# One encoder layer on one core: the second norm's sums one product later, two additions of a down visit on GpSimd, one scaling tied in VectorE's order

## The chip, the core and the metric

The kernel runs on one core of a Trainium2 chip. A core has TensorE (matmuls, results in the eight PSUM banks), VectorE (DVE in the profile), ScalarE (ACT), GpSimd (POOL) and SyncE (SP, which here only issues transfers); each works through its own queue in order, and they wait for one another by semaphores. The metric is the device time of one execution in microseconds (us); the time of a kernel is the median of its runs.

## The reference

One layer of an encoder on 1024 tokens of width 1024, in float32: a norm, a projection, a pooling mixer beside chunked attention, an output projection; then a norm, a gated MLP of width 2816, and a gated input embedding; a last norm. The part that the change touches is the MLP:

```python
hn = rmsnorm(h, norm_ffn_g[i])          # y * rsqrt(mean(y*y) + EPS) * g
up = hn @ w_up[i]                       # (1024, 1024) @ (1024, 2 * 2816)
gt, val = up[..., :D_FF], up[..., D_FF:]
gt = causal_dwconv(gt, conv_w[i], conv_b[i])
h = h + (jax.nn.gelu(gt, approximate=False) * val) @ w_down[i]
```

## The kernel before, in words

**Layout.** Features lie on the 128 partitions, tokens along the free axis. The residual is H[0] to H[7], eight tiles of 128 features by 1024 tokens; HS[0] and HS[1] are the two halves of 512 tokens. Every float32 operand of a matmul is kept as a high part (ScalarE writes it, L141, in a rounded format) and a low part (VectorE writes the rest, L142), and each product is three matmuls (mm3, L136 to L138): high by high, high by low, low by high. `split` is this pair of operations.

**Up projection.** Block fi (0 to 21) is 128 gate columns and 128 value columns of w_up. Its four sub-products (gate or value, first or second token half) over the two halves of the input features are computed with seven products in place of eight, numbered 1 to 7, from sums and differences of the weight halves (`summed`, L893) and of the activations (forms). `step(fi, n)` runs product n: twelve matmuls into one of the banks x, y, z, w, then what must be read from it. For blocks 0 and 1 the banks are firsts[0] = (0, 3, 5, 4) and firsts[1] = (2, 3, 1, 5). Product 1 leaves its result in bank x; `seed` (L984, ScalarE) copies it, negated, into bank y as the start of products 6 and 7, and product 2 then goes on accumulating in bank x. After product 3 the gate's convolution follows: L1005 and L1006 on VectorE, the taps of L1031 on ScalarE, L1034 and L1035 on VectorE, then GELU on ScalarE (L1036). After product 7 VectorE takes one half of the values from PSUM (L1013), after product 4 the other (L1016, the scaling: values times the norm's factor). `product` splits the weights of three products ahead, into a ring of three buffers, so the split for product i + 3 waits until product i has been run.

**The second norm.** Its factor for a token is a power of the mean square. `Norm.add` squares a tile on ScalarE and adds it up on VectorE (L815), `sums` adds over the partitions with four matmuls by a column of ones (L821; the profile lists eight records), followed by a small VectorE operation (L824) and a power on GpSimd (L825); `rows` turns the result into rows with four transposes on TensorE (L829). norm_a is that of the first token half, norm_b of the second. The last squares of norm_b are added up when the output projection ends, directly ahead of the first up products, which are written at L1057 to L1063: (0,1), (1,1), norm_b.sums(), (0,2), (0,5). norm_b.rows() is called after product (0,3).

**Down projection.** It is done in groups g of four blocks, also with seven products, numbered 1, 2, 5, 4, 6, 7, 3 in their order. Each is called a visit here: `down_next` runs 24 matmuls into banks 4 to 7, adds the four results to the residual (L1236), and has the next visit's operands split (`split_next`; where the sign is negative by `split_last`, L1187 on ScalarE and L1188 on VectorE). Visits are hooked between the products of `up`. Their operands are sums and differences of gated tiles, which SyncE loads into buffers "one" and "grow" from memory (L1165) and GpSimd's transfers accumulate onto (L1163). Visit (4,5) falls into block 20, after product 3. Before its matmuls two additions (L1227, one for each of its j) add the "grow" tiles, of which (4,5) has already split its parts, onto the "one" tiles, the raw operands of the next visit, (4,4). The accumulating transfers into "grow" for visit (4,6) come after these reads. (4,4) is run in block 21, after product 1; between (4,5) and it lie the products (20,4) and (21,1).

**What sets the order.** TensorE's order is that of the program (`manual_schedule`). In this part of the kernel the other engines' orders are made when the kernel is built, by a planner that gives each engine the first ready instruction in the order of writing, by its own estimate of times; `high_priority(AHEAD)` moves an instruction 60 places forward in that order. `keep_in_program_order(i)` ties instruction i behind the last instruction written for its engine before it. The additions L1227 are tied this way, and so are the splits of (4,4), except for the high parts L1187.

Of the kernel before, what the change touches and what calls it, by code (L numbers as in the profile page):

```python
# [9 lines left out]
ALU = mybir.AluOpType  # L10
# [91 lines left out]
def trunk(tc, x0, xT, xn, pT, vecs, w_qk0, w_in, w_v, bias, counts, pool_w, w_out, w_up, w_down,  # L102
          w_gate, w_ple, out):
    nc = tc.nc
    act, dve, pe, pool, sp = nc.scalar, nc.vector, nc.tensor, nc.gpsimd, nc.sync

    with tc.tile_pool(name="sb", bufs=1) as sb, \
# [8 lines left out]
        PS = pp.tile([P, 8, 512], F32, name="PS")  # L116
# [6 lines left out]
        def r(kb, n):  # L123
            if kb >= 128:
                return B[:, int((kb - 128) * KW):int((kb - 128) * KW) + n]
            return R[:, int(kb * KW):int(kb * KW) + n]

        def f(kb, n):
            return F[:, int(kb * KW):int(kb * KW) + n]
# [4 lines left out]
        def mm3(ps, ahi, alo, bhi, blo, first, last, more=False):  # L134

            pe.matmul(ps, ahi, bhi, start=first, stop=False, skip_group_check=more)  # L136
            pe.matmul(ps, ahi, blo, start=False, stop=False, skip_group_check=more)  # L137
            pe.matmul(ps, alo, bhi, start=False, stop=last, skip_group_check=more)  # L138
# [22 lines left out]
        V = r(64, 8192).rearrange("p (k h c) -> p k h c", k=NTOK, h=N_HEADS)  # L161
# [623 lines left out]
        HS = [slice(0, 512), slice(512, 1024)]  # L785
# [59 lines left out]
        V = v_pool.__enter__().tile([P, SEQ], F32, name="V")  # L845
# [16 lines left out]
        rst = f(44, SEQ)  # L862
# [63 lines left out]
        def product(bank, first):  # L926

            i = done[0]
            prepare(i + 1)
            form = forms[order[i][1]]  # L930
            w_ = wu[i % 3]
            for k in range(4):
                mm3(PS[:, bank], w_[:, 0, k], w_[:, 1, k], *form[k], first and k == 0, k == 3, not first)
            done[0] += 1
            prepare(i + 4)
# [42 lines left out]
        def keep(dst, bank, scale=1.0):  # L978
            with tc.high_priority(AHEAD):
                act.activation(dst, PS[:, bank], AF.Copy, scale=scale)  # L980

        def seed(to, bank, scale=1.0):
            with tc.high_priority(AHEAD):
                act.activation(PS[:, to], PS[:, bank], AF.Copy, scale=scale)  # L984

        def step(fi, n):

            x, y, z, w = firsts.get(fi, (0, 1, 2, 3))
            product({1: x, 2: x, 5: z, 3: z, 6: y, 7: y, 4: w}[n], n in (1, 5) or n == 4 and fi < 2)
            if n == 1 and fi != 1:  # L990
                seed(y, x, -1.0)
            elif n == 2 and fi:
                gate0(x)
                if fi in halved[1:]:
                    gate(fi, HS[0])
            elif n == 5:
                keep(p5, z)
            elif n == 6:
                keep(u2, y)
                if fi == 1:  # L1000
                    gate(fi, HS[0], True)
            elif n == 3:
                if fi == 0:
                    norm_b.rows(rst[:, HS[1]])
                dve.tensor_tensor(G2, PS[:, z], u2, ALU.subtract)  # L1005
                dve.tensor_tensor(G2, G2, rst[:, HS[1]], ALU.mult)  # L1006
                gate(fi, HS[1] if fi in halved else slice(0, SEQ))
            elif n == 7:
                if fi > 1:
                    seed(w, y)  # L1010
                else:
                    keep(V[:, HS[0]], y)
                dve.tensor_tensor(V[:, HS[1]], PS[:, y], p5, ALU.subtract)  # L1013
            elif n == 4:
                if fi > 1:
                    dve.tensor_tensor(V[:, HS[0]], PS[:, w], rst[:, HS[0]], ALU.mult)  # L1016
                else:
                    dve.tensor_tensor(V[:, HS[0]], PS[:, w], V[:, HS[0]], ALU.add)
                    dve.tensor_tensor(V[:, HS[0]], V[:, HS[0]], rst[:, HS[0]], ALU.mult)

        def gate0(bank):
            dve.tensor_tensor(Gb[:, 2:2 + 512], PS[:, bank], rst[:, HS[0]], ALU.mult)

        def gate(fi, ts, pinned=False):

            a, b = ts.start, ts.stop
            y = Yb[:, ts]

            def cw(j):
                return vec[:, C_CW + j * NF + fi:C_CW + j * NF + fi + 1]  # L1030
            taps = act.activation(y, Gb[:, 2 + a:2 + b], AF.Identity, bias=vec[:, C_CB + fi:C_CB + fi + 1], scale=cw(2))  # L1031
            if pinned:
                tc.keep_in_program_order(taps)
            dve.scalar_tensor_tensor(y, Gb[:, 1 + a:1 + b], cw(1), y, ALU.mult, ALU.add)  # L1034
            dve.scalar_tensor_tensor(y, Gb[:, a:b], cw(0), y, ALU.mult, ALU.add)  # L1035
            act.activation(y, y, AF.Gelu)  # L1036
# [17 lines left out]
        def store(dst, ts=slice(0, SEQ)):  # L1054
            split(Yb[:, ts], dst[:, ts], dst[:, 1024 + ts.start:1024 + ts.stop])

        step(0, 1)  # L1057
        step(1, 1)
        norm_b.sums()
        step(0, 2)  # L1060
        for k in range(4):
            put(3, k, b22[k])
        step(0, 5)  # L1063
# [53 lines left out]
        raws, pairs = {}, {}  # L1117
# [77 lines left out]
        def split_next(pinned=False, held_back=False):  # L1195
            if nsplit[0] == len(sequence) or nsplit[0] > ndown[0]:
                return
            g, n = sequence[nsplit[0]]
            if not all((side, g, n) in asked for side in "wa"):
                return  # L1200
            nsplit[0] += 1
            pinned = pinned or (g, n) == (4, 4)
            for side in "wa":
                sign = -1.0 if side == "a" and n in NEGATIVE else 1.0
                for j in range(2):
                    t = raws[side, buffer(side, n), j]
                    hi, lo = pairs[side, j]
                    if sign > 0:
                        split(t, hi, lo, pinned)
                    else:  # L1210
                        last_piece.append((side, g, n, j, pinned))
                        if not (held_back and j):
                            split_last()
                if not last_piece:
                    split_done.add((side, g, n))
            ask()

        def down_next():

            g, n = sequence[ndown[0]]  # L1220
            ndown[0] += 1
            assert nsplit[0] == ndown[0]
            if (g, n) == (4, 5):
                assert ("a", 4, 4) in asked
                for j in range(2):
                    t = raws["a", "one", j]
                    tc.keep_in_program_order(dve.tensor_tensor(t, t, raws["a", "grow", j], ALU.add))  # L1227
            fresh = n in (1, 5, 6, 7)
            for d in range(4):
                for j in range(2):  # L1230
                    (whi, wlo), (ahi, alo) = pairs["w", j], pairs["a", j]
                    ds_ = slice(d * P, (d + 1) * P)
                    mm3(PS[:, 4 + d], whi[:, ds_], wlo[:, ds_], ahi, alo, fresh and j == 0, j == 1, not fresh)
                to, h = {1: (4, 1), 5: (4, 1), 6: (4, 1), 7: (4, 1), 2: (0, 0), 4: (4, 0), 3: (0, 1)}[n]
                t = H[to + d][:, HS[h]]
                dve.tensor_tensor(t, t, PS[:, 4 + d], ALU.subtract if n in (1, 5) else ALU.add)  # L1236
            if n == 1 and g < 4:
                put_off[0] = 3
            else:
                split_next()  # L1240
# [306 lines left out]
```

## Time and profile before

| what | value |
|---|---|
| median of 3 runs | 1113.71 us (1113.18 to 1114.12) |
| the profiled execution | 1113.26 us |
| its span, first to last instruction | 1111.5 us |
| TensorE clock granted | 0.998 |
| TensorE busy | 1103.6 us, 99% |
| VectorE busy | 846.9 us, 76% |
| ScalarE busy | 579.4 us, 52% |
| GpSimd busy | 166.3 us, 15% |

The profile is of one execution. All times of the views are microseconds from the first instruction. A row of a timeline has the start, the duration, the engine, the line of the kernel, the operation with its result and inputs (R, BQ and TB hold operands in SBUF, F and RW float32 tiles in SBUF, PS is PSUM, Yd the gated tiles in memory), the shape, and in brackets how long the engine stood idle before it and who ended that. Matmuls overlap: one is shown as 0.39 us long, but they start about 0.23 us apart, so time on TensorE is read from start to start. The spans of GpSimd are rough.

### The profile page before, as it was taken

The numbers are of one execution on the slowest core, as the hardware profiler recorded it, in microseconds if no ns is written. First come the engines' busy times: TensorE is split into PE (matmuls) and PEld (weight loads), VectorE is DVE, ScalarE is ACT, GpSimd is POOL, SyncE is SP. The second block draws the span as 40 slices with busy tenths as digits, with TensorE's granted clock in tenths as the row PEclk, the third lists the DMA queues.
The fourth block names the chain that finished last, engine by engine and source line by source line (L and its number), as shares of the span: only waits on it lengthen the run. The fifth ranks groups of instructions, "written<-read, shape, count | busy, mean of one in ns | idle before, by whom it ended". The sixth has DMA issues, their size and how long they took to land.

```text
span 1111.5 us, 15629 instructions
## 1 busy us (share of the span) xinstructions
PE 1103.6 (99%) x5651; PEld 918.5 (83%) x5651; DVE 846.9 (76%) x1435; ACT 579.4 (52%) x1022; POOL 166.3 (15%) x211
## 2 busy tenths in 40 slices
PE   9999999999999999999999999999999999999997
PEld 7888888888888888888888888888888888888887
DVE  6437767788678888788788778777887789986845
ACT  7537767756656544444344444434434445674534
POOL 0000201285022100310131012101220112000000
PEclk9999999999999999999999999999999999999999
DMA  9401111123500543864576457645684566320003
GB/s 349 163 1 44 40 43 40 42 68 104 190 29 1 150 116 134 175 136 141 146 174 144 141 148 167 163 135 159 155 178 133 142 161 142 124 95 20 1 35 117
DMA packets 66317, 129.03 MB, mean 116 GB/s; under 512 B 7488, under 2 KB 9408, under 8 KB 66240
## 3 DMA queue, kind: packets, MB, share of 16 engines
q1 hardware_dynamic: 51696, 101.82, 27.8%
q0 software_dynamic: 13824, 25.17, 13.8%
q8 instruction: 44, 0.72, 0.3%
q10 hardware_dynamic: 720, 1.05, 0.3%
q14 instruction: 33, 0.27, 0.1%
HBM read 112.02 MB, written 14.68 MB: 114 GB/s over the span
## 4 chain that ended last, share of the span: by engine, by line
PE 94%; DVE 2%; issue 2%; POOL 1%; ACT 1%; DMA 0%; POOLq 0%; DVEq 0%; ACTq 0%
PE PS L136 29%; PE PS L137 29%; PE PS L138 29%; PE PS L504 3%; PE PS L428 2%; PE PS L451 2%; DVE R L142 1%; PE PS L821 0%; POOL F L958 0%; ACT R L141 0%; DMA F<-in_x 0%; DVE F L1270 0%; DVE F L950 0%; PE PS L212 0%; POOL small L825 0%
## 5 line engine op out<-in xcount | busy, mean ns | idle before, releaser
L136 PE MATMUL PS<-R 128*128 128x512 f32 (+1 forms) x1084 | 419.8, 387 | 0.0
L138 PE MATMUL PS<-R 128*128 128x512 f32 (+1 forms) x1084 | 416.8, 385 | 0.0
L137 PE MATMUL PS<-R 128*128 128x512 f32 (+1 forms) x1084 | 416.8, 384 | 0.0
L136 PEld LDWEIGHTS PS<-R 128*128 128x128 f32 x1084 | 203.7, 188 | 42.9 <-issue 2.9
L138 PEld LDWEIGHTS PS<-R 128*128 128x128 f32 x1084 | 203.7, 188 | 40.7
L137 PEld LDWEIGHTS PS<-R 128*128 128x128 f32 x1084 | 203.7, 188 | 39.7
L141 ACT ACTIVATE R<-F 128x512 fp32r<-128x512 f32 (+2 forms) x220 | 137.0, 638 | 186.9 <-PE PS L137 89.5
L142 DVE TENSOR_TENSOR R<-F,R 128x512 fp32r<-128x512 f32 (+2 forms) x220 | 154.5, 717 | 48.9 <-ACT R L141 48.0
L1236 DVE TENSOR_TENSOR F<-F,PS 128x512 f32<-128x512 f32 x140 | 92.6, 680 | 7.2 <-PE PS L138 6.9
L141 ACT ACTIVATE BQ<-RW 128x512 fp32r<-128x512 f32 x90 | 52.6, 622 | 82.8 <-PE PS L137 78.8
L893 DVE TENSOR_TENSOR F<-F 128x512 f32<-128x512 f32 x88 | 60.5, 687 | 44.1 <-DMA F<-in_w_up 42.0
L1163 POOL DMA_DIRECT2D RW<-Yd x56 | 49.7, 892 | 258.7 <-DMA RW<-Yd 202.6
L1163 POOL DMA_DIRECT2D RW<-in_w_down x40 | 35.8, 952 | 231.9 <-DMA RW<-in_w_down 193.5
L142 DVE TENSOR_TENSOR BQ<-RW,BQ 128x512 fp32r<-128x512 f32 x90 | 59.0, 683 | 3.1 <-PE PS L137 2.6
L137 PE MATMUL PS<-BQ 128*128 128x512 f32 x140 | 54.6, 390 | 0.1
L136 PE MATMUL PS<-R,BQ 128*128 128x512 f32 x140 | 54.5, 389 | 0.0
L138 PE MATMUL PS<-BQ 128*128 128x512 f32 x140 | 54.5, 389 | 0.0
L137 PE MATMUL PS<-R,BQ 128*128 128x512 f32 x140 | 54.5, 389 | 0.0
L138 PE MATMUL PS<-R,BQ 128*128 128x512 f32 x140 | 54.5, 389 | 0.0
L136 PE MATMUL PS<-BQ 128*128 128x512 f32 x140 | 54.5, 389 | 0.0
L405 ACT ACTIVATE F<-F,small 128x640 f32<-128x640 f32 (+4 forms) x64 | 44.0, 689 | 13.0 <-DVE small L393 11.6
L1031 ACT ACTIVATE F<-F,vec 128x1024 f32<-128x1024 f32 (+1 forms) x25 | 28.6, 1142 | 41.2 <-DVE F L1006 39.9
(177 smaller groups left out, 1577.9 us busy)
## 6 DMA issues: line engine op xcount, KB each, us to landing
F<-in_w_up SPq DMA_DIRECT2D x91, 256.0 KB, 3.9
RW<-Yd POOLq DMA_DIRECT2D x56, 256.0 KB, 5.2
RW<-Yd SPq DMA_DIRECT2D x55, 256.0 KB, 4.0
RW<-in_w_down SPq DMA_DIRECT2D x50, 256.0 KB, 2.8
RW<-in_w_down POOLq DMA_DIRECT2D x40, 256.0 KB, 6.2
Yd<-F SPq DMA_DIRECT2D x40, 256.0 KB, 3.5
F<-in_w_in SPq DMA_DIRECT2D x10, 512.0 KB, 3.5
F<-in_xn SPq DMA_DIRECT2D x8, 512.0 KB, 7.8
```

The costliest lines, as they stand in the source:

```text
L136: pe.matmul(ps, ahi, bhi, start=first, stop=False, skip_group_check=more)
L137: pe.matmul(ps, ahi, blo, start=False, stop=False, skip_group_check=more)
L138: pe.matmul(ps, alo, bhi, start=False, stop=last, skip_group_check=more)
L141: both = (act.activation(hi, src, AF.Copy), dve.tensor_tensor(lo, src, rv(hi), ALU.subtract))
L142: dve.tensor_tensor(lo, src, rv(hi), ALU.subtract))
L405: push(1.9 + 0.85 * z, lambda S=S, s_=s_: act.activation(S, S, AF.Exp, bias=s_[:, 0:1], scale=-1.0, accum_out=s_[:, 1:2]))
L428: pe.matmul(PS[:, places[x][y], place[1]:place[1] + wide], q[halves[x], t * P:(t + 1) * P], k[halves[x], ki + y * wide:ki + (y + 1) * wide ...
L504: pe.matmul(Os[j][:, (a - t0) * P:(b - t0) * P].rearrange("p (t q) -> p t q", q=P), V[:, k, 2 * c_ + j], PT[part][:, b0:b0 + by * (b - a - ...
L893: return dve.tensor_tensor(rawu[to], rawu[a], rawu[b], op)
L1031: taps = act.activation(y, Gb[:, 2 + a:2 + b], AF.Identity, bias=vec[:, C_CB + fi:C_CB + fi + 1], scale=cw(2))
L1163: pool.dma_start(t, src, accum_op=ALU.add)
L1236: dve.tensor_tensor(t, t, PS[:, 4 + d], ALU.subtract if n in (1, 5) else ALU.add)
```

## The change

Three edits. The sums of norm_b are called after product (0,2) instead of before it. The two additions ahead of visit (4,5) go from VectorE to GpSimd, with the same tie, now behind GpSimd's last written instruction. The scaling L1016 of block 20 is tied behind VectorE's last written instruction, which is the low part of the weights of product (21,6), written when product (20,4) is done.

```diff
             elif n == 4:
                 if fi > 1:
-                    dve.tensor_tensor(V[:, HS[0]], PS[:, w], rst[:, HS[0]], ALU.mult)
+                    i = dve.tensor_tensor(V[:, HS[0]], PS[:, w], rst[:, HS[0]], ALU.mult)
+                    if fi == 20:
+                        tc.keep_in_program_order(i)
...
         step(0, 1)
         step(1, 1)
+        step(0, 2)
         norm_b.sums()
-        step(0, 2)
...
                 for j in range(2):
                     t = raws["a", "one", j]
-                    tc.keep_in_program_order(dve.tensor_tensor(t, t, raws["a", "grow", j], ALU.add))
+                    tc.keep_in_program_order(pool.tensor_tensor(t, t, raws["a", "grow", j], ALU.add))
```

## The prediction

> **What bounds the kernel now.** I read the page first. Its span and its row of TensorE:
>
> ```profile
> span 1111.5 us, 15629 instructions
> PE 1103.6 (99%) x5651; PEld 918.5 (83%) x5651; DVE 846.9 (76%) x1435; ACT 579.4 (52%) x1022; POOL 166.3 (15%) x211
> ```
>
> TensorE is busy 99% of the span and its order is the program's, so a change to other engines is worth only what it does to a gap of TensorE. The second view is the list of waits of the weight loads (each matmul loads its weights just before it): line that waited, who ended the wait, total, times, longest.
>
> ```profile
> PEld PS L137 <- DVE BQ L1188: 0.6, 1, 0.6
> PEld PS L821 <- DVE F L815: 0.5, 1, 0.5
> ```
>
> Each of these two gaps lies at a place that the change touches: L821 is the sums of the second norm, L1188 the low part of the visit (4,4) that follows the two additions (L1227). Together they are about one microsecond, 0.1% of the run. A measurement of this kernel can tell about 0.2% (2.2 us) from no change, so removing both completely would not show; only a new loss could.
>
> **Part 1, the sums one product later.** The timeline of TensorE (start, duration, line) and that of ScalarE around the gap:
>
> ```profile
> 358.94 0.39 PE L137 MATMUL PS<-R 128*128 128x512 f32 x1
> 359.17 0.39 PE L138 MATMUL PS<-R 128*128 128x512 f32 x1
> 359.61 1.05 PE L821 MATMUL PS<-small,F 128*128 128x1 f32 x8
> 360.53 0.48 PE L136 MATMUL PS<-R 128*128 128x512 f32 x1
> 360.85 0.39 PE L137 MATMUL PS<-R 128*128 128x512 f32 x1
> ```
>
> ```profile
> 357.85 0.63 ACT L813 ACTIVATE F<-F 128x512 f32<-128x512 f32 x1 [1.41 <-DVE F L950]
> ...
> 359.52 0.57 ACT L984 ACTIVATE PS<-PS 128x512 f32<-128x512 f32 x1
> ```
>
> Matmuls of the stream start 0.23 us apart (358.94, 359.17). 359.17 is the last of product (1,1); twelve matmuls earlier, at 356.4, the last of (0,1) started, and its bank is complete at about 356.8. Without a wait the next would start at 359.40; the sums start at 359.61, a wait of 0.21, and the second matmul of (0,2) at 360.85, so its first has the regular slot 360.62. Wait and sums cost 360.62 - 359.40 = 1.22 us. What do sums cost that need not wait? The first norm's:
>
> ```profile
> 314.45 0.95 PE L821 MATMUL PS<-small,F 128*128 128x1 f32 x8
> 315.26 0.49 PE L136 MATMUL PS<-R 128*128 128x512 f32 x1
> 315.58 0.40 PE L137 MATMUL PS<-R 128*128 128x512 f32 x1
> ```
>
> By the same rule 315.58 - 0.23 - 314.45 = 0.90 us. So 0.32 us is there to win, if nothing is late next. But something is: the product that moves up is (0,2), and it accumulates into bank 0, where (0,1) left its result. step(0,1) asked for a copy of that result into bank 3 (seed, L984), and (0,2) may not write before the copy has read. L984 is the last ScalarE row above: it stands in ScalarE's queue behind L813, which waited 1.41 us for VectorE, and ends at 359.52 + 0.57 = 360.09. Today that is hidden, since (0,2) starts at 360.53. With the sums moved, (0,2) would be called at 359.40 and wait until about 360.14 (the 0.05 of handover that L821 shows after L815): 0.74 us, some 0.11 to get back into step (a waiting matmul's successor comes 0.34 instead of 0.23 us later, as at 927.44 below), and the sums still cost 0.90 behind it. 1.75 against 1.22: **0.5 us slower**. The lower end is -0.3 (the copy is queued before L813, when (0,1) is done), the upper 0.6. I take 0.5, because nothing in the move changes what ScalarE is given or in which order it is written. The rest of the norm's chain moves with the sums, which then end near 363.9: a small VectorE operation (L824), and right behind it GpSimd's power. L824 now runs just before 363.93, so it would hold VectorE's queue for some tenths of a microsecond; what stands in that queue has 1.61 us to spare, the wait at 371.78:
>
> ```profile
> 363.93 1.44 POOL L825 TENSOR_TENSOR small<-small 128x4 f32<-128x4 f32 x1 [9.72 <-DVE small L824]
> ```
>
> ```profile
> 371.78 0.69 DVE L1005 TENSOR_TENSOR F<-PS,F 128x512 f32<-128x512 f32 x1 [1.61 <-PE PS L138]
> ```
>
> TensorE wants the power's result only at L829, behind three products (36 matmuls, 8.2 us): nothing.
>
> **Part 2, the two additions on GpSimd.** VectorE before and after them, then ScalarE, then TensorE:
>
> ```profile
> 913.95 0.69 DVE L142 TENSOR_TENSOR R<-F,R 128x512 fp32r<-128x512 f32 x1 [0.31 <-ACT R L141]
> 914.56 0.68 DVE L1013 TENSOR_TENSOR V<-PS,F 128x512 f32<-128x512 f32 x1
> 915.16 0.68 DVE L893 TENSOR_TENSOR F<-F 128x512 f32<-128x512 f32 x1
> ...
> 921.75 1.27 DVE L1035 SCALAR_TENSOR_TENSOR F<-F,vec 128x1024 f32<-128x1024 f32 x1
> 922.95 1.28 DVE L1227 TENSOR_TENSOR RW<-RW 128x512 f32<-128x512 f32 x2
> 924.15 0.68 DVE L1236 TENSOR_TENSOR F<-F,PS 128x512 f32<-128x512 f32 x1
> 924.89 0.69 DVE L142 TENSOR_TENSOR R<-F,R 128x512 fp32r<-128x512 f32 x1
> 925.50 1.28 DVE L142 TENSOR_TENSOR BQ<-RW,BQ 128x512 fp32r<-128x512 f32 x2
> 926.71 0.68 DVE L1188 SCALAR_TENSOR_TENSOR BQ<-RW,BQ 128x512 fp32r<-128x512 f32 x1
> ```
>
> ```profile
> 923.06 1.06 ACT L1036 ACTIVATE F<-F 128x1024 f32<-128x1024 f32 x1 [3.54 <-DVE F L1035]
> 924.23 0.63 ACT L141 ACTIVATE R<-F 128x512 fp32r<-128x512 f32 x1
> ```
>
> ```profile
> 926.91 0.39 PE L136 MATMUL PS<-BQ 128*128 128x512 f32 x1
> 927.44 0.50 PE L137 MATMUL PS<-BQ 128*128 128x512 f32 x1
> ...
> 928.71 0.39 PE L136 MATMUL PS<-BQ 128*128 128x512 f32 x1
> ```
>
> Six intervals from 926.91 to 928.71 should take 1.36 us and take 1.80: the gap costs 0.44. What the removal gives: VectorE has 1.20 us less to do (922.95 to 924.15) and L1236 moves up. But the next, L142 at 924.89, needs the high part that ScalarE writes at 924.23, done at 924.86. ScalarE gets to it only after L1036, which waited 3.54 us for L1035. So the low parts hang on L1035, L1036, two kinds of L141 and their own chain, in which the additions are no link: L142 starts at 924.89 with or without them. **Gain 0**; at most 0.44 if ScalarE's or VectorE's order comes out otherwise.
>
> What the addition costs: when does GpSimd do it? Each is tied behind GpSimd's last written instruction, the transfer of 912.85, and needs the second accumulating load of its tile.
>
> ```profile
> 907.14 0.86 POOL L1163 DMA_DIRECT2D RW<-Yd  x1 [1.26 <-issue]
> ...
> 912.85 0.87 POOL L1163 DMA_DIRECT2D RW<-in_w_down  x1 [0.31 <-issue]
> ```
>
> ```profile
> RW<-Yd POOLq DMA_DIRECT2D x2, 256.0 KB, 6.7
> ```
>
> 907.14 + 6.7 = 913.8, and 912.85 + 0.87 = 913.7. So they run from about 913.8, when VectorE begins a stretch without a gap that leads to L1035. How GpSimd and VectorE get along on such tiles, the trace shows elsewhere:
>
> ```profile
> 352.90 1.30 POOL L958 TENSOR_TENSOR F<-TB 128x512 f32<-128x512 f32 x1 [2.63 <-ACT TB L939]
> ```
>
> ```profile
> 353.31 1.44 DVE L142 TENSOR_TENSOR R<-TB,R 128x512 fp32r<-128x512 f32 x1 [0.44 <-ACT R L141]
> ```
>
> ```profile
> 247.30 0.68 DVE L600 TENSOR_TENSOR F<-PS,F 128x512 f32<-128x512 f32 x1
> 247.90 1.04 DVE L539 TENSOR_TENSOR B<-F,B 128x512 fp32r<-128x512 f32 x1
> ```
>
> ```profile
> 246.95 0.73 POOL L628 TENSOR_TENSOR F<-F 128x256 f32<-128x256 f32 x1
> 247.76 2.81 POOL L614 TENSOR_TENSOR F<-F 128x269 f32<-128x269 f32 x3
> ```
>
> GpSimd's addition of this size takes 1.30 us. A VectorE operation with two SBUF inputs that meets it takes 1.44 instead of 0.68, ending 0.55 after GpSimd's end (354.20): it stands still meanwhile. L600, with an input from PSUM, keeps its 0.68 beside GpSimd, and L539 right after it does not. Now the stretch: the first addition holds L142 (913.95) until 915.10, so it ends at 915.65. The second addition follows; L1013 reads PSUM and runs beside it; L893 waits until 916.95 and ends at 917.50 instead of 915.84. That is 1.65 us late (much the same if VectorE gets in first), and there is no gap before L1035 to take it up. L1035 then ends 1.65 later, so L1036, the high parts and L1188 too, less the 0.05 that L141 stood after L1036: **1.6 us slower** at 927.44. The lower end is 0 (no meeting), or -0.44 with a luckier order; the upper 2.3, if all VectorE work stops for both (2.6, less the 0.31 of idle at 913.95).
>
> The Trainium skill has this as a rule (SBUF — State Buffer, "SBUF: two separate sides"): the port pair that the two engines share is locked for a whole instruction, against a VectorE operation with two SBUF inputs if GpSimd's reads SBUF. The rows agree, the stop of 353.31 as well as the free run of 247.30. By it the sum is the 1.6; by the price of the additions on VectorE alone it would be 0. Another page (Perfetto Trace Analysis, "Optimizing Scalar/DVE Operations") says that moving work between the two may not help, which speaks against this edit.
>
> Behind the additions on GpSimd stand the transfers into the tile that they read; they go out earlier than before and nobody waits for them there.
>
> **Part 3, the tie.** The scaling L1016 of block 20 may not pass the low part written just before it, the L142 of 924.89. It runs well after it today:
>
> ```profile
> 928.51 0.68 DVE L1016 TENSOR_TENSOR V<-PS,F 128x512 f32<-128x512 f32 x1
> ```
>
> Its input, the product that ends at 924.2, is ready before, so without the additions it could come early; the tie only excludes the place ahead of L142. Cost 0; up to 0.6 (its spacing) if it is put between L142 and the low parts of 925.50.
>
> **The sum.** 0.5 + 1.6 + 0 = 2.1 us. The profiled execution took 1113.26 us, 1.8 more than its span; the median of the runs is 1113.71, 0.45 above it. 1113.26 + 2.1 = 1115.4 for a profiled execution, 1115.8 on the scale of the median.
>
> **Rivals.** (a) Neither loss: ScalarE copies bank 0 early, and the order of the low parts improves by the freed VectorE. -0.3 and -0.44: 1113.0. For it: both gaps are waits of TensorE on exactly the work that is moved or lightened. Against: L984's end, and the lock. (b) The additions do no harm (they fall beside operations that read PSUM, or the order of VectorE is other), the sums do: 1114.2. (c) The reverse, -0.3 + 1.6: 1115.0. (d) Clearly slower: both losses, and the scaling slips between L142 and the low parts, where each microsecond is TensorE's: 2.1 + 0.6, 1116.4. It decides when the scaling's input is in the planner's clock ready before the first high part of (4,4); on the chip the two are close (924.2, and the high part a little before L142 ends at 925.5). Against: the low parts are written first. (e) The change does not do what it says: if GpSimd's additions ran only after 922.95, the low parts would wait for 2.6 us of additions instead of 1.2; they are not tied to that, so I give it no place of its own.
>
> **Chances.** Forecast 0.45, (a) 0.23, (b) 0.13, (c) 0.07, (d) 0.10, 0.02 for an order that comes out much better. A third of the forecast's spread lies over 1115.94, the 0.2% bound: slower 0.15 + 0.10 = 0.25; faster 0.02; same 0.73. The range takes (a) to (d), 1112.9 to 1116.5; the forecast's own is 1115.4 to 1116.2.
>
> **What would show it.** In the new profile: no wait of L821 on L815, but one of the first matmul of (0,2), released by L984, of about 0.7 us; L1227 as two GpSimd rows of 1.3 us near 914 to 917, a VectorE row of some 1.7 at 914; L1035 ending near 924.7 plus the 0.5 of part 1; the wait on L1188 about 2 us long. It is wrong if L984 ends by 359.4, if VectorE's rows at 914 keep 0.68, or if the low parts start before 925.5 on the old scale.

## The result, and the profile after

| | before | after |
|---|---|---|
| median of ten runs each | 1113.70 us (1113.03 to 1114.40) | 1116.55 us (1115.62 to 1117.53) |
| profiled execution | 1113.26 us | 1117.53 us |
| its span | 1111.5 us | 1115.8 us |

The ratio is 1.0027, 95% interval 1.0018 to 1.0035: the change makes the kernel 2 to 4 us slower. The line numbers of after are two higher than before's behind L1016 (L1227 is L1229, L1188 is L1190, L1035 and L1036 are L1037 and L1038).

The page of after, its row of TensorE. It counts 2.4 us more as busy than before, though the matmuls are as many:

```profile
PE 1106.0 (99%) x5651; PEld 920.2 (82%) x5651; DVE 848.3 (76%) x1433; ACT 579.1 (52%) x1022; POOL 168.4 (15%) x213
```

The list of waits of the weight loads. L821's wait for L815 is gone, as foreseen; a wait for the seed's copy L984 and one for the high part of (4,4), L141, have come, and the wait for the low part has grown from 0.6 to 1.8:

```profile
PEld PS L137 <- DVE BQ L1190: 1.8, 1, 1.8
...
PEld PS L136 <- ACT PS L984: 0.9, 1, 0.9
PEld PS L136 <- ACT BQ L141: 0.8, 1, 0.8
```

The timeline of TensorE at the two places (start, duration, line):

```profile
359.34 0.39 PE L138 MATMUL PS<-R 128*128 128x512 f32 x1
360.23 0.50 PE L136 MATMUL PS<-R 128*128 128x512 f32 x1 [0.50 <-ACT PS L984]
360.57 0.40 PE L137 MATMUL PS<-R 128*128 128x512 f32 x1
...
363.12 0.95 PE L821 MATMUL PS<-small,F 128*128 128x1 f32 x8
...
364.25 0.40 PE L137 MATMUL PS<-R 128*128 128x512 f32 x1
...
927.35 0.39 PE L138 MATMUL PS<-R 128*128 128x512 f32 x1
928.08 0.50 PE L136 MATMUL PS<-BQ 128*128 128x512 f32 x1 [0.34 <-ACT BQ L141]
930.09 0.50 PE L137 MATMUL PS<-BQ 128*128 128x512 f32 x1 [1.51 <-DVE BQ L1190]
930.42 0.48 PE L138 MATMUL PS<-BQ 128*128 128x512 f32 x1
930.70 0.63 PE L136 MATMUL PS<-R,BQ 128*128 128x512 f32 x1
931.12 0.63 PE L137 MATMUL PS<-R,BQ 128*128 128x512 f32 x1
...
934.07 0.39 PE L138 MATMUL PS<-R,BQ 128*128 128x512 f32 x1
```

Three losses are to be read here.

- The first, at 360. The second matmul of (0,2) starts at 360.57, its regular place would be 359.34 + 2 x 0.23 = 359.80: 0.77. The sums cost 364.25 - 0.23 - 363.12 = 0.90 behind it. 1.67 against 1.22 before: 0.45 us lost.
- The second, at 928, where now the high part of the visit (L141) is late as well as the low part. From 927.35 the third matmul of the visit should start 3 x 0.23 = 0.69 later, at 928.04, and starts at 930.42: 2.4 us, where before lost 0.44. Loss 1.95.
- The third was not in the prediction: behind the gap matmuls start up to 0.43 us apart instead of 0.23. The nine intervals from 930.42 to 934.07 take 3.65 us, and at 0.23 they would take 2.05. Loss 1.6.

The sum is 4.0, of the 4.3 by which the two spans differ; 0.17 of the rest had come about before 359 (359.17 is 359.34 here). What the third loss is, the view of stretches tells (from:to, length, then busy time of PE, PEld, DVE, ACT and POOL, the granted clock, DMA share, GB/s):

```profile
932.00:933.00 1.00, 1.00 (x4) 0.81 (x3) 0.78 (x2) 0.00 (x0) 0.81 (x2) 0.50 1.02 209
...
934.00:936.00 2.00, 2.00 (x10) 1.60 (x10) 0.84 (x3) 1.06 (x1) 0.60 (x1) 1.00 1.06 238
```

TensorE's granted clock is 0.50 after the gap and 1.00 again from 934. A row of PE that is "busy" all the time hides this: the count in brackets, 4 a microsecond and then 5, shows it.

Where does the second loss come from? GpSimd's additions and VectorE's rows from 914 on, then ScalarE's at both places:

```profile
914.07 2.87 POOL L1229 TENSOR_TENSOR RW<-RW 128x512 f32<-128x512 f32 x2
```

```profile
914.61 2.89 DVE L142 TENSOR_TENSOR R<-F,R 128x512 fp32r<-128x512 f32 x1 [0.31 <-ACT R L141]
917.42 0.68 DVE L1013 TENSOR_TENSOR V<-PS,F 128x512 f32<-128x512 f32 x1
...
924.62 1.27 DVE L1037 SCALAR_TENSOR_TENSOR F<-F,vec 128x1024 f32<-128x1024 f32 x1
```

```profile
359.59 0.58 ACT L984 ACTIVATE PS<-PS 128x512 f32<-128x512 f32 x1
...
925.92 1.06 ACT L1038 ACTIVATE F<-F 128x1024 f32<-128x1024 f32 x1 [2.50 <-DVE F L1037]
...
927.41 1.14 ACT L141 ACTIVATE BQ<-RW 128x512 fp32r<-128x512 f32 x2
```

ScalarE's copy L984 ends at 359.59 + 0.58 = 360.17, and (0,2) starts right behind it, at 360.23. For the second loss: L142 was at 913.95 before and is at 914.61 now, 0.66 later (the 0.17 and part 1). It lasts 2.89 instead of 0.69: it stands still through both additions. L1013 starts at 917.42, 2.86 later than before, and L1037 at 924.62, 2.87 later. Of that, 0.66 was there before, so the additions cost 2.2 us of VectorE's order. Nothing of it is made good in the following seven microseconds, and ScalarE passes it on, less 0.2, to the high and the low parts of (4,4).

### The profile page after: what moved, and what is told of

Same layout as the page of the kernel before. It is cut to its first block, busy times and chain, and to the rows that moved or that the text cites. A ratio compares the mean times of both kernels' runs of the same rounds, so it can differ in the third digit from the quotient of the medians.

```text
span 1115.8 us, 15627 instructions
## 1 busy us (share of the span) xinstructions
PE 1106.0 (99%) x5651; PEld 920.2 (82%) x5651; DVE 848.3 (76%) x1433; ACT 579.1 (52%) x1022; POOL 168.4 (15%) x213
## 4 chain that ended last, share of the span: by engine, by line
PE 94%; DVE 2%; issue 2%; ACT 1%; POOL 1%; POOLq 0%; DVEq 0%; ACTq 0%
PE PS L136 29%; PE PS L137 29%; PE PS L138 29%; PE PS L504 3%; PE PS L428 2%; PE PS L451 2%; DVE R L142 1%; ACT R L141 0%; PE PS L821 0%; POOL F L958 0%; PE PS L226 0%; PE PS L212 0%; DVE F L950 0%; DVE F L1272 0%; POOL small L825 0%
## 5 line engine op out<-in xcount | busy, mean ns | idle before, releaser
L141 ACT ACTIVATE R<-F 128x512 fp32r<-128x512 f32 (+2 forms) x220 | 137.1, 638 | 193.0 <-PE PS L137 86.1
L142 DVE TENSOR_TENSOR R<-F,R 128x512 fp32r<-128x512 f32 (+2 forms) x220 | 157.3, 729 | 52.1 <-ACT R L141 51.2
L141 ACT ACTIVATE BQ<-RW 128x512 fp32r<-128x512 f32 x90 | 52.6, 622 | 83.6 <-PE PS L137 79.5
L893 DVE TENSOR_TENSOR F<-F 128x512 f32<-128x512 f32 x88 | 60.5, 688 | 41.2 <-DMA F<-in_w_up 38.2
L142 DVE TENSOR_TENSOR BQ<-RW,BQ 128x512 fp32r<-128x512 f32 x90 | 59.1, 685 | 3.0 <-PE PS L137 2.1
```

The source lines that it names most:

```text
L141: both = (act.activation(hi, src, AF.Copy), dve.tensor_tensor(lo, src, rv(hi), ALU.subtract))
L142: dve.tensor_tensor(lo, src, rv(hi), ALU.subtract))
L893: return dve.tensor_tensor(rawu[to], rawu[a], rawu[b], op)
```

## The experiments

Each kernel was timed against the one before on the same chip; ratios have their 95% interval. "Dropped" counts executions whose mean granted clock was 0.997 or less; of the 80 executions of the kernel before that were timed beside the experiments there was one, and it took 1113.82 us. A value of 0.997 alone is thus not proof of a lost microsecond.

**The sums alone** (only the first edit).

```diff
         step(1, 1)
+        step(0, 2)
         norm_b.sums()
-        step(0, 2)
```

> Only the first edit (sums of the second norm after product (0,2)). Theory: (0,2) has to wait for the copy out of bank 0, so the wait of L821 (0.48 us in the list of waits) is replaced by one of the first matmul of (0,2) on L984; the run gets 0.5 us longer, 1114.2, with a gap near 359.4 to 360.2. Rival (the move itself is harmless, the whole loss sits at the visit): 1113.7 or 0.3 less, no wait on L984.

Measured: 1114.13 us against 1113.31, ratio 1.0006 (0.9997 to 1.0015), none of 11 dropped. Its list of waits has the wait for L984, and that for L1188 unchanged at 0.6:

```profile
PEld PS L136 <- ACT PS L984: 0.9, 1, 0.9
```

The time alone does not settle half a microsecond; the row does: this edit alone brings the wait, at its full 0.9.

**The sums, with the copy reading another bank.** The copy of (0,1) reads bank 7 in place of bank 0, so that (0,2) need not wait for it; with that, block 0's products 6 and 7 begin from another start.

```diff
-                seed(y, x, -1.0)
+                seed(y, x if fi else 7, -1.0)
```

> The first edit alone, with the copy of product (0,1) (L984) reading bank 7 instead of bank 0, so that block 0 gets a wrong start for its products 6 and 7, and nothing else is left out. Theory: with no reader of bank 0 the product (0,2) runs on without a wait, the wait of L821 on L815 is gone too, and the run is 0.3 us shorter than the kernel before: 1113.0. Rival (something else holds (0,2) at 359.4, its weights or its forms): the gap stays near 0.7 us, 1114.1.

Measured: 1113.29 us against 1113.60, ratio 0.9998 (0.9989 to 1.0007). TensorE goes on in step where it waited, and the sums run behind the product:

```profile
359.19 0.39 PE L138 MATMUL PS<-R 128*128 128x512 f32 x1
359.41 0.39 PE L136 MATMUL PS<-R 128*128 128x512 f32 x1
...
362.13 0.94 PE L821 MATMUL PS<-small,F 128*128 128x1 f32 x8
```

So it is the bank that (0,2) waits for. The gain that the edit would have without it, 0.3, is below what the times can tell.

**The other two edits** (additions on GpSimd, and the tie), and **the additions without the tie**:

```diff
-                    tc.keep_in_program_order(dve.tensor_tensor(t, t, raws["a", "grow", j], ALU.add))
+                    tc.keep_in_program_order(pool.tensor_tensor(t, t, raws["a", "grow", j], ALU.add))
```

> The second and third edit without the first. Theory: GpSimd holds both additions back to back, VectorE's row at 914 becomes 2.9 us long, TensorE loses 2.4 us instead of 0.44 at the visit (4,4), and in part of the executions TensorE's clock is halved for some 3.5 us after that gap, 1.6 us more: 1115.7 where the clock stays, up to 1117.3 where it doesn't, and single runs spread over that. Rival (the clock drop needs the other gap at 360 as well, or has nothing to do with the gap): 1115.7 throughout, with a spread as that of the kernel before.

> The second edit alone, without the tie: the planner then puts the scaling L1016 ahead of the low parts. Theory: the scaling takes a place of 0.6 us on VectorE, but VectorE has time there while it waits for ScalarE behind the late L1035, so TensorE's gap is the same or up to 0.6 us longer than with the tie: 1115.7 to 1117.8. Rival (the tie itself is what costs): 1113.7, no gap over 0.5 us.

Measured with the tie: 1115.83 us against 1113.31, ratio 1.0024 (1.0015 to 1.0032). The eleven executions fall in two groups: six from 1114.84 to 1115.83, and five dropped ones from 1116.57 to 1117.54. The profiled one is of the first group. Its TensorE:

```profile
926.80 0.39 PE L138 MATMUL PS<-R 128*128 128x512 f32 x1
927.53 0.50 PE L136 MATMUL PS<-BQ 128*128 128x512 f32 x1 [0.34 <-ACT BQ L141]
929.54 0.50 PE L137 MATMUL PS<-BQ 128*128 128x512 f32 x1 [1.51 <-DVE BQ L1190]
929.87 0.39 PE L138 MATMUL PS<-BQ 128*128 128x512 f32 x1
930.10 0.39 PE L136 MATMUL PS<-R,BQ 128*128 128x512 f32 x1
```

The gap is the same to the hundredth as in after (0.73 and 2.01 from start to start), and here matmuls go on at 0.23. After, which differs by the first edit only, lost 1.6 us more behind the same gap in its profiled execution. The second loss belongs to these edits. That the third does too is read from the granted clock of the five dropped executions; none of them was profiled.

Measured without the tie: 1117.03 us, ratio 1.0031 (1.0019 to 1.0042), three of six dropped. The planner put the scaling ahead of the low part (VectorE):

```profile
926.11 0.68 DVE L1016 TENSOR_TENSOR V<-PS,F 128x512 f32<-128x512 f32 x1
926.71 0.67 DVE L142 TENSOR_TENSOR R<-F,R 128x512 fp32r<-128x512 f32 x1
```

and TensorE stopped a third time, for the fifth matmul. Reckoned to the sixth, the gap grew by 0.6 (from 926.45 to 930.79 takes 4.34, six regular intervals 1.36, so 2.98 against the 2.39 with the tie). The tie prevents this; no run has the tie without the additions.

**Low parts first**: the additions stay on VectorE; the one split of weights that ScalarE takes between L1036 and the high parts of (4,4), that of product (21,6), is put behind them, with its low part on VectorE.

```diff
-                with tc.high_priority(AHEAD):
-                    split(rawu[t].rearrange("p (k c) -> p k c", k=4), w_[:, 0], w_[:, 1])
+                if (fi, n) == (NF - 1, 6):
+                    split(rawu[t].rearrange("p (k c) -> p k c", k=4), w_[:, 0], w_[:, 1], True)
+                else:
+                    with tc.high_priority(AHEAD):
+                        split(rawu[t].rearrange("p (k c) -> p k c", k=4), w_[:, 0], w_[:, 1])
```

> The kernel before, with only the split of the weights of product (21,6) put behind the high parts of visit (4,4) on ScalarE. Theory: the low parts of (4,4) hang on ScalarE's order, not on the additions, so with the additions still on VectorE the wait on L1188 (0.6 us in the list of waits) is gone and the run is 0.4 us shorter, 1113.3; not to be told from 1113.7 by the times alone, but by the gap at 927. Rival (the additions are the link): the wait stays at 0.6.

Measured: 1113.04 us against 1113.31, ratio 0.9999 (0.9990 to 1.0008). TensorE has no gap at (4,4):

```profile
927.94 0.39 PE L138 MATMUL PS<-R 128*128 128x512 f32 x1
928.16 0.39 PE L136 MATMUL PS<-BQ 128*128 128x512 f32 x1
928.39 0.39 PE L137 MATMUL PS<-BQ 128*128 128x512 f32 x1
```

The gap of before goes away with both additions still on VectorE ahead of the low parts. So the order behind L1036 is enough to make or close it. That unloading VectorE alone would win nothing is still the prediction's argument: no run takes the additions off VectorE without putting them on GpSimd. (In this execution, of 1114.08 us, another visit's low part is late, at 890.18; the run with one addition on GpSimd shows the same wait.)

**One addition on GpSimd**, the other on VectorE, with the tie. It tells whether each addition has its price.

```diff
-                    tc.keep_in_program_order(dve.tensor_tensor(t, t, raws["a", "grow", j], ALU.add))
+                    tc.keep_in_program_order((dve if j else pool).tensor_tensor(t, t, raws["a", "grow", j], ALU.add))
```

> The third edit, and only the first of the two additions on GpSimd; the second stays on VectorE. Theory: VectorE's row at 914 is some 1.6 us long instead of 0.69, L1035 comes 1.0 us late, TensorE loses about 1.4 us at (4,4) instead of 0.44, and the clock drops less often than with both: 1114.3, with few runs over 1115.5. Rival (any addition on GpSimd brings the whole loss): 1115.8.

Measured: 1114.62 us against 1113.60, ratio 1.0010 (1.0001 to 1.0018), none of 11 dropped. VectorE:

```profile
915.21 1.65 DVE L142 TENSOR_TENSOR R<-F,R 128x512 fp32r<-128x512 f32 x1 [0.30 <-ACT R L141]
```

TensorE's low-part wait is 1.4 there, between the 0.6 of before and the 1.8 of after. One addition holds L142 for one microsecond (1.65 less 0.69), both for 2.2.

**Does VectorE get a turn between the additions?** Two kernels put something between them on GpSimd: a fill of one column that is tied to nothing, and a multiplication by ones of one column of the second tile, which the second addition must wait for.

```diff
                     tc.keep_in_program_order(pool.tensor_tensor(t, t, raws["a", "grow", j], ALU.add))
+                    if j == 0:
+                        tc.keep_in_program_order(pool.memset(small[:, 3:4], 0.0))
```

> The second and third edit, with a one-column memset on GpSimd between the two additions. Theory of the back-to-back hold: the memset opens a gap in which VectorE gets its turn, so its row at 914 is 1.6 us long, the operation from PSUM runs beside the second addition, and another row is lengthened; L1035 comes 1.65 us late instead of 2.2, 0.5 us less than with the additions back to back: 1115.3. Rival (GpSimd's waiting instruction always wins): the row stays 2.9 us, 1115.8.

```diff
                     tc.keep_in_program_order(pool.tensor_tensor(t, t, raws["a", "grow", j], ALU.add))
+                    if j == 0:
+                        t = raws["a", "one", 1][:, 0:1]
+                        tc.keep_in_program_order(pool.tensor_tensor(t, t, ones, ALU.mult))
```

> The second and third edit, with a one-column operation of GpSimd between the two additions that multiplies a column of the second tile by one, so that the second addition has to wait for its end. Theory (VectorE gets its turn only where GpSimd itself waits): the row of VectorE at 914 is some 1.6 us long instead of 2.9, a later one is lengthened, L1035 comes 1.65 us late instead of 2.2, and the wait on the low part L1190 is 0.5 us shorter: 1115.3 where the clock stays. Rival (VectorE's waiting operation always loses while GpSimd has work): the row stays near 2.9 us, 1115.8.

The fill: 1116.76 us against 1113.60, ratio 1.0028 (1.0018 to 1.0038), six of nine dropped. GpSimd, then VectorE:

```profile
913.45 1.63 POOL L1229 TENSOR_TENSOR RW<-RW 128x512 f32<-128x512 f32 x1
...
914.84 1.52 POOL L1229 TENSOR_TENSOR RW<-RW 128x512 f32<-128x512 f32 x1
```

```profile
913.99 2.93 DVE L142 TENSOR_TENSOR R<-F,R 128x512 fp32r<-128x512 f32 x1 [0.30 <-ACT R L141]
```

My expectation missed, the rival's came. The second addition starts at 914.84, before the first ends at 913.45 + 1.63 = 915.08: the fill separates nothing. The chained one: 1115.49 us against 1113.43, ratio 1.0018 (1.0009 to 1.0027), one of 11 dropped.

```profile
913.84 1.62 POOL L1229 TENSOR_TENSOR RW<-RW 128x512 f32<-128x512 f32 x1
915.19 0.86 POOL L1232 TENSOR_TENSOR RW<-RW,small 128x1 f32<-128x1 f32 x1
916.13 1.29 POOL L1229 TENSOR_TENSOR RW<-RW 128x512 f32<-128x512 f32 x1
```

```profile
914.37 1.65 DVE L142 TENSOR_TENSOR R<-F,R 128x512 fp32r<-128x512 f32 x1 [0.31 <-ACT R L141]
915.94 0.68 DVE L1013 TENSOR_TENSOR V<-PS,F 128x512 f32<-128x512 f32 x1
916.54 1.43 DVE L893 TENSOR_TENSOR F<-F 128x512 f32<-128x512 f32 x1
```

These are nearly the rows that the prediction had written down for the change itself: L142 for 1.65 (1.70 there), L1013 beside the second addition, L893 held until its end. L142 starts 0.42 later than before and L1037, at 923.89, 2.14 later, so the additions cost 1.72, where 1.65 was expected. The wait on the low part was expected 0.5 shorter and is still 1.8; the half microsecond is saved just ahead of it, where the first matmul of (4,4) now starts 0.24 behind its neighbour (927.35) instead of 0.73.

The run shows that VectorE can get a turn between the two additions. It does not show why. L142 ends at 914.37 + 1.65 = 916.02, that is 0.56 behind the end of the first addition (915.46), so it had its turn right there, ahead of the multiplication's end at 916.05. The multiplication does not use the first addition's result, and starts before that has ended. And the trace of after has another place where GpSimd runs two operations in a row, neither of which uses the other's result (L968 changes b21, L958 takes b12 from b11):

```profile
328.50 1.29 POOL L968 TENSOR_TENSOR TB<-TB 128x512 f32<-128x512 f32 x1 [9.97 <-DVE R L142]
329.75 1.74 POOL L958 TENSOR_TENSOR F<-TB 128x512 f32<-128x512 f32 x1
```

```profile
329.64 0.70 DVE L893 TENSOR_TENSOR F<-F 128x512 f32<-128x512 f32 x1 [1.22 <-DMA F<-in_w_up]
```

VectorE's L893, which the second addition holds up in the chained kernel, ends here at 330.34, 0.55 behind the end of the first GpSimd operation (329.79), and it is the second GpSimd operation that takes 0.45 longer than the first. So VectorE can get a turn without any tie between the two GpSimd operations, and what decides who is next stays open.

**Is it GpSimd that lowers the clock, or TensorE's gap?** The kernel before, with no addition on GpSimd, and four (then two) extra operations of 0.6 us on VectorE behind the additions. The extra operations change no value.

```diff
+                for z in range(4):
+                    t = raws["a", "one", z % 2]
+                    tc.keep_in_program_order(dve.tensor_tensor(t, t, t, ALU.max))
```

> The kernel before with four more operations of 0.6 us on VectorE behind the two additions (each the maximum of a tile with itself), nothing on GpSimd. Theory of the clock: TensorE's gap at (4,4) becomes some 2.4 us longer, 1116.1 where the clock stays, and in part of the executions it is halved for some 3.5 us after the gap, up to 1117.8, with a granted clock of 0.996 or 0.997 over the run. Rival (the drop belongs to GpSimd's additions, not to the gap): 1116.1 with the spread of the kernel before and a clock of 0.998 or more throughout.

> As the run with four more operations on VectorE, but with two: TensorE's gap at (4,4) is some 2.0 us instead of 3.2. Theory (the clock drops when a gap is long enough, at a moment that varies): 1115.2 where the clock stays, and a clock below 0.998 in fewer executions than with the longer gap, or in none. Rival (any stop at this place brings it): as many as with the longer gap.

With four: 1117.86 us against 1113.60, ratio 1.0035 (1.0022 to 1.0047), three of five dropped. TensorE of the profiled one, and one stretch of its view of stretches:

```profile
926.62 0.40 PE L136 MATMUL PS<-BQ 128*128 128x512 f32 x1
930.01 0.79 PE L137 MATMUL PS<-BQ 128*128 128x512 f32 x1 [2.99 <-DVE BQ L1188]
930.60 0.63 PE L138 MATMUL PS<-BQ 128*128 128x512 f32 x1
931.03 0.63 PE L136 MATMUL PS<-R,BQ 128*128 128x512 f32 x1
...
936.15 0.41 PE L136 MATMUL PS<-R,BQ 128*128 128x512 f32 x1
```

```profile
932.00:934.00 2.00, 2.00 (x6) 1.53 (x5) 1.49 (x2) 1.06 (x1) 1.77 (x2) 0.50 0.93 316
```

The clock is 0.50 without any addition on GpSimd, so it follows the gap. With two, I expected fewer drops than with four, or none, and that missed; the rival's, as many, came. Measured: 1116.49 us against 1113.43, ratio 1.0025 (1.0016 to 1.0034), and 8 of 11 dropped (1116.31 to 1116.92; the others 1114.83 to 1115.61). Its gap:

```profile
926.78 0.39 PE L136 MATMUL PS<-BQ 128*128 128x512 f32 x1
928.97 0.50 PE L137 MATMUL PS<-BQ 128*128 128x512 f32 x1 [1.80 <-DVE BQ L1188]
```

**Both gaps of before taken away**: low parts first, and two VectorE operations that stood ahead of the last square's L815 held behind it.

```diff
-                        dve.tensor_tensor(a, a, b, op)
+                        if d == 3:
+                            with tc.issue_after(norm_b.newest.ins):
+                                dve.tensor_tensor(a, a, b, op)
+                        else:
+                            dve.tensor_tensor(a, a, b, op)
```

> The kernel before with the split of product (21,6) put behind the high parts of (4,4), and with the two residual operations of L1270 for the last tile held behind the last addition L815 of the second norm. Theory: L815 ends 0.6 us earlier, L821 no longer waits, and the gap at (4,4) is gone: 0.3 + 0.4 = 0.7 us shorter than before, 1112.9. Rival (other work of VectorE is late instead): one of the two waits stays, or a new one stands near 360 to 372, and 1113.3 or more.

Measured: 1113.19 us (1112.47 to 1113.95) against 1113.43, ratio 0.9995 (0.9986 to 1.0004). One further execution of the eleven took 2647.53 us; nothing here shows why, and the range leaves it out. Both waits are gone from its list, and no difference can be told by the time: by the prediction's sums, 0.32 + 0.44 = 0.8 us was all that the two places had.

## Why the prediction was wrong

The direction was right, and so were the two mechanisms that it named, the wait for the copy and the engines that shut each other out; the time is 0.75 us above the 1115.8 forecast and 0.05 above the end of the range, and the loss is larger than 0.2%, to which the prediction gave one chance in four.

- **Part 1, 0.5: right.** The new wait is for L984, as the prediction put it, and costs 0.45 with the sums. Shown by the sums alone and by the other bank. L825's rows behind it disturbed nothing.
- **The gain of the additions, 0: not contradicted.** Low parts first shows that the gap of before hangs on the order behind L1036; the additions taken off VectorE at no price were not run.
- **The cost of the additions, 1.6: the step that failed.** It read: "it ends at 915.65. The second addition follows; L1013 reads PSUM and runs beside it; L893 waits until 916.95". The mechanism, GpSimd and VectorE shutting each other out, is the right one, but the step gave VectorE a turn between the two additions. It got none: 2.89 us in one row, 2.2 of delay instead of 1.65, 1.95 on TensorE instead of 1.6. The prediction had this case as its upper bound, 2.3, and took the lower value from a trace (353.31) where a single addition met a single operation. With one addition on GpSimd, L142 is held for that one only, and the chained additions give nearly the predicted rows; so what the step had wrong is the turn between the two. The Trainium skill (SBUF — State Buffer, "SBUF: two separate sides") says that whoever starts first has the port pair for the whole instruction. The rows agree for each instruction. They do not agree among themselves on who is next (914.61 against 329.64), and that was the question. A small slip goes the other way: L141 at 924.23 stood 0.11 behind the end of L1036 (924.12), not 0.05, and in after it starts 0.09 before that end, so that 0.2 of the delay was made good there.
- **A term that was missing: the clock, 1.6 in part of the executions.** The prediction counted a gap of TensorE at its length. In the profiled execution it costs 1.6 more behind it. The median of after lies between executions without this loss (1115.62 is the lowest, and 1113.7 + 0.45 + 1.95 = 1116.1) and with it (1117.33 to 1117.53, four of ten). So of the 0.75 that the forecast was short, about 0.3 is the hold; the rest is put down to this term.
- **Part 3, 0: right.** Its absence costs 0.6; the rival in which the scaling slips in was a danger of the additions alone, and the tie closes it. That this rival's time, 1116.4, is close to the measured one is chance: its mechanism does not occur.

Open is what decides whether the clock drops in a given execution, what gives VectorE its turn between two GpSimd operations, and whether the executions of after at 0.997 or less and the three from 1116.29 to 1116.75 at 0.998 are long and short forms of one thing; no run here was profiled in both forms on one kernel.

## What to carry to other kernels

Before an operation is moved from VectorE to GpSimd, look at what VectorE does at that moment. With float32 tiles in SBUF on both, VectorE's operation stood still here until GpSimd's had ended: 1.0 us for one addition, 2.2 for two in a row. Count on no turn between two in a row unless a trace of the same place shows it. Ask whether the operation is a link of the chain that ends late at all; here the order of one other split was, and putting that split later closed the gap without any move. In a kernel that keeps TensorE at 99%, price a gap of about 2 us at its length and, in part of the executions, 1.6 us again.

## What the runs showed of the hardware

**The clock after a short gap.** Longest stretch without a start of a matmul at (4,4), less the regular 0.23, in the profiled execution, and dropped executions:

| kernel | idle, us | dropped |
|---|---|---|
| one addition on GpSimd | 1.11 (928.17 to 929.51) | 0 of 11 |
| chained additions | 1.78 | 1 of 11 |
| after | 0.50 and, one matmul later, 1.78 | 4 of 10 |
| additions and tie | 0.50 and 1.78 | 5 of 11 |
| additions with the fill | 0.54 and 1.78 | 6 of 9 |
| additions without the tie | 0.49 and 1.85 | 3 of 6 |
| two extra operations | 1.96 | 8 of 11 |
| four extra operations | 3.16 | 3 of 5 |

Of these profiled executions only those of after and of four extra operations were dropped ones; for the others the gap of the dropped executions is not known. With 1.78 us alone one execution of 11 dropped, and with a stop of 0.5 just ahead of it 15 of 30. The one dropped execution of the chained additions, at 1115.78 us, was no longer than its neighbours. A longer stretch did not bring more drops here (8 of 11 at 1.96, 3 of 5 at 3.16).

With four extra operations the clock fell while TensorE still stood: it is 0.83 from 928 to 930 and 0.50 from 930 to 936, so half the clock began at about 929.3 (an estimate from these values). In after it is 0.80 from 930 to 931 and 0.50 from 931 to 934, so it began at about 930.6, half a microsecond after matmuls had started again at 930.09. It lasted to about 936 and 934. Matmuls then start 0.43 apart, and 0.23 otherwise. The Trainium skill (TensorE: Matmul & The Clock Gate, "Why this matters for your kernels") warns of idle gaps over about 3 us. Here the trace of after shows the drop behind stops of 0.50 and 1.78 us, and the measurement decides.

**GpSimd's own times.** In these rows the next instruction starts before the one ahead of it has ended, unless it depends on it: the second of two additions at 914.84 with the first ending at 915.08, but the chained one at 916.13, behind 915.19 + 0.86 = 916.05. An addition of 128x512 is shown as 1.29 to 1.63 us, two in a row as 2.87.
